# Hybrid GDN/SSD decoder layer in float32: the first SSD group's gate projection is traced amid the keys, the first pair's z projection amid that group's x tiles

## The chip, the cores and the metric

The kernel runs on one core of a Trainium2 chip. A core has a matrix engine (TensorE, PE in the profile; PEld are its weight loads), a vector engine (VectorE, DVE), an activation engine (ScalarE, ACT), GpSimd (POOL), a queue engine (SyncE, SP) that issues the transfers, and 16 DMA engines. The metric is the device time of one execution in microseconds (us).

## The reference, cut to what matters

One decoder layer, batch 1, 1024 tokens, width 1024, all float32. One input projection feeds two token mixers side by side.

```
h = rms_norm(x, pre_mix_norm)
q, k, v, z_a, b_a, a_a, z_s, x_s, b_s, c_s, dt_s = split(h @ w_in)      # 8 GDN heads, 16 SSD heads in 2 groups
q, k, v = silu(causal_conv4(q|k|v)); q, k = l2norm(q)*dk**-0.5, l2norm(k)
o_a = rms_norm(gdn_chunked(q, k, v, g, beta)) * silu(z_a)               # delta rule: a triangular solve per chunk
x_s, b_s, c_s = silu(causal_conv4(x_s|b_s|c_s) + bias)
y = (ssd_chunked(x_s, dt, -exp(a_log), b_s, c_s) + d * x_s) * silu(z_s) # chunked scan, per group
x = x + rms_norm(concat(o_a, rms_norm(y)) @ w_out, post_mix_norm)
h = rms_norm(x, pre_ffn_norm)
gate, up = split(causal_conv3(h @ w_up) + bias)
x = x + rms_norm((silu(gate) * up) @ w_down, post_ffn_norm)
```

## The kernel before

**Projections.** Tokens are done in two halves of 512 (`half`). Every large product is made of three passes: weights and activations are split into a rounded part (`hi`) and a rest (`lo`), and `product3` (L138 to 142) issues hi times hi, hi times lo and lo times hi. One projection of 128 channels over 512 tokens (`project`) is 8 row blocks times 3, so 24 matmuls of 512 columns. `weights` loads 512 KB (SP), makes `whi` (ACT, L127) and `wlo` (DVE, L128; two pieces each); these instructions are traced with a priority that lies 100 places ahead. `conv_proj` is a projection followed by the causal convolution (`conv`, L248: three DVE instructions, and three of ACT around them). `rowwise` is the other form: four accumulators, one for each 128 tokens, and 512 channels at once, so 96 matmuls and four loads of 512 KB. It has no convolution.

**Order.** A main stream (`in_projections`) runs as a generator. Each `yield` of the stream lets every waiting side task (a list `tasks`) go on by one step: that is a round. Between two yields the stream traces 6 or 9 large matmuls. The side tasks are `k_tok` and `k_inner` (inner products of a pair's keys), `solve` (inversion of the 32 by 32 diagonal blocks, 31 steps of two DVE instructions, L602 and L604, after all four pairs of keys went through DRAM), `ssd_chain` (the SSD group's scan over four chunks), `pair_chain` (a head pair's delta rule over four chunks). `wait(n)` lets n rounds pass. The framework then orders each engine's instructions by priority, which is the order of tracing, but lets a later instruction come forward when, by its own planning, an engine would stand idle and the later one has its operands and buffers. Each engine then executes its list in that fixed order.

**The stream of a half**, before: eight key projections (`keys`, four pairs); then the first SSD group: B, C, four x tiles, and last its gate z (`rowwise`, 512 channels, silu at L802); then the head pairs: q and v of pair 0; q of pair 1, the z projection of pair 0 (`pair_z`, two projections, silu at L658), v of pair 1; z of pair 1; the second SSD group; pairs 2 and 3 likewise. `ssd_chain` is put on the list behind the fourth x tile, before the gate projection is traced.

**Buffers that matter.** Accumulators `acc`: 5 PSUM banks (the gate takes 4 at once); `psm`: 3 PSUM banks for everything small; `kq`: 4 (B and C of a group take one, each head one); `sz` (silu of z): 2, one pair's worth; `xrow`: 4 (the gate takes 2); three `wraw`, and `whi` and `wlo` for two projections. A pair's `sz` is freed when its `pair_chain` has ended (`o.over`), the group's `kq` buffer when its chain has read C for the last time.

Of the kernel before, what the change touches and what calls it, by code (L numbers as in the profile page):

```python
# [39 lines left out]
def hybrid_layer_kernel(  # L40
# [247 lines left out]
    def wait(n):  # L288
        for _ in range(n):
            yield  # L290
# [5 lines left out]
    with ExitStack() as actx:  # L296
# [207 lines left out]
                self.ready = 0  # L504
                self.solved = False

        def keys(h, half, gt, ps):

            ks = Keys()
            pairs = []  # L510
            for pair in range(HG // 2):
                o = Work()
                o.half, o.gt, o.pair, o.ks = half, gt, pair, ks
                o.heads = (2 * pair, 2 * pair + 1)
                o.ssk = sp.tile([P, 2, NC], F32, name="ssk", bufs=4)
                o.nk = sp.tile([P, 2, NC], F32, name="nk", bufs=5)
                o.kt, o.kx = [], [None, None]
                for i, hd in enumerate(o.heads):
                    t = ap.tile([P, T], F32, tag="kT", name="kT", bufs=3)
                    o.kt.append(t)  # L520
                    yield from conv_proj(h, half, COL_K + hd * P, 8 + hd,
                                         [gcw[:, tt, 8 + hd:9 + hd] for tt in range(4)], None, t, ps)
                    ps = None
                    nc.sync.dma_start(ks.kt[hd], t)
                    tasks.append(k_tok(o, i))
                tasks.append(k_inner(o))
                pairs.append(o)
                if half == 0 and pair == 1:
                    empty_images()
            tasks.append(solve(ks))  # L530
            return pairs

# [81 lines left out]
        def pair_q(o, h):  # L614
            ks = o.ks
            o.eq = sp.tile([P, 2, NC], F32, name="eq")
            o.kq, o.ktok, o.sz, o.vt = [], [], [None, None], [None, None]
            o.done = 0
            o.qd = ap.tile([P, 2, NC, P], F32, tag="qd", name="qd", bufs=2)
            for i, hd in enumerate(o.heads):  # L620
                t = ap.tile([P, 2, T], F32, tag="kq", name="kq", bufs=4)
                o.kq.append(t)
                nc.sync.dma_start(t[:, 0, :], ks.kt[hd])
                kx = ap.tile([P, NC, P], F32, tag="ktok", name="ktok", bufs=5)
                nc.sync.dma_start(kx, ks.tok[hd].rearrange("p (c n) -> p c n", c=NC))
                o.ktok.append(kx)
                nc.sync.dma_start(o.qd[:, i], ks.dec[hd].rearrange("p (c n) -> p c n", c=NC))
                yield from conv_proj(h, o.half, COL_Q + hd * P, hd,
                                     [gcw[:, tt, hd:hd + 1] for tt in range(4)], None, t[:, 1, :])
                tasks.append(q_tok(o, i))  # L630
# [146 lines left out]
            o.over = True  # L777


        def ssd_group(h, half, gt, g):  # L780
            o = Work()
            o.half, o.gt, o.g = half, gt, g
            o.bc = ap.tile([P, 2, T], F32, tag="kq", name="bc", bufs=4)
            o.xt = ap.tile([P, NC, 512], F32, tag="b8", name="xt", bufs=1)
            for j, (col, cb) in enumerate(((COL_B, 8), (COL_C, 10))):
                ci = cb + g
                yield from conv_proj(h, half, col + g * P, 24 + ci, [scw[:, tt, ci:ci + 1] for tt in range(4)],
                                     scb[:, ci:ci + 1], o.bc[:, j, :])
            tasks.append(b_tok(o))
            for ct in range(4):  # L790
                ci = 4 * g + ct
                xc = yield from conv_proj(h, half, COL_X + ci * P, 24 + ci,
                                          [scw[:, tt, ci:ci + 1] for tt in range(4)], scb[:, ci:ci + 1], None)
                tasks.append(x_tok(o, ct, xc))
            o.zt = None
            tasks.append(ssd_chain(o))
            zt = [xp.tile([P, 2, 512], F32, tag="xrow", name="zt") for _ in range(NC // 2)]
            zt = [zt[c // 2][:, c % 2, :] for c in range(NC)]
            pz = accumulators()
            yield from rowwise(pz, KD, lambda k: (h[0][k], h[1][k]),  # L800
                               lambda k: w_in[k * P:(k + 2) * P, COL_ZS + g * 512:COL_ZS + (g + 1) * 512],
                               lambda c: S_.activation(zt[c], pz[c], AF.Silu))  # L802
            o.zt = zt
# [14 lines left out]
        def ssd_chain(o):  # L818
# [40 lines left out]
            for c in range(NC):  # L859
                L, xdt, xdd = now  # L860
                cl = slice(c * P, (c + 1) * P)
                zero = half == 0 and c == 0
                if not zero:
                    po = bank()
                    PE.matmul(po, bc[:, 1, cl], St[g], start=True, stop=True)
                    yo = ap.tile([P, 512], F32, tag="ch", name="yo", bufs=2)
                    V.tensor_tensor(heads(yo), heads(po), per_head(gt["eg"], c, 64), ALU.mult)
                    V.tensor_tensor(xt[:, c, :], xt[:, c, :], yo, ALU.add)
                if not (half == NH - 1 and c == NC - 1):
                    pn = bank()  # L870
                    PE.matmul(pn, o.bt[:, c, :], xdd, start=True, stop=True)  # L871
                    if zero:
                        V.tensor_copy(St[g], pn)
                    else:
                        V.tensor_tensor(heads(St[g]), heads(St[g]), per_head(gt["el"], c, 64), ALU.mult)
                        V.tensor_tensor(St[g], St[g], pn, ALU.add)
                yield
                yield from wait(W["s2"])
                pd = bank()
                for hh in range(8):  # L880
                    PE.matmul(pd[:, hh * 64:(hh + 1) * 64], L[:, hh, :], xdt[:, hh * 64:(hh + 1) * 64],  # L881
                              start=True, stop=True)
                V.tensor_tensor(xt[:, c, :], pd, xt[:, c, :], ALU.add)
                if c + 1 < NC:
                    now = prepare(c + 1)
                yield
                yield from wait(W["s3"])
            while o.zt is None:
                yield
            yield from wait(W["zt"])  # L890
# [20 lines left out]
        def in_projections(half, rows, w):  # L911

            pg = acc.tile([P, T], F32, tag="acc", name="acc")
            ps = acc.tile([P, T], F32, tag="acc", name="acc")
            g64 = pg[:2 * NG, :]

            def use(k, hi, lo):
                a, z = k == 0, k == KD - 1
                if a:
                    PE.matmul(g64, wga[:, k, :], hi[k], start=True, stop=False)  # L920
                PE.matmul(pg[:NG, :], wga[:, k, :NG], lo[k], start=False, stop=False)
                if not a:
                    PE.matmul(g64, wga[:, k, :], hi[k], start=False, stop=z)
                product3(ps, w[k][0], w[k][1], hi[k], lo[k], a, z)

            h = yield from transposed(rows, wmix, use)
            nonlocal gcw
            if gcw is None:
                gcw = columns(gcw_rows, "colB")
                gcw = gcw.rearrange("p (t c) -> p t c", c=24)  # L930
            gt = {}
            tasks.append(gates(g64, gt, half))
            yield
            pairs = yield from keys(h, half, gt, ps)
            yield from ssd_group(h, half, gt, 0)
            before = None
            for step in (0, 1, "s1", 2, 3):
                if isinstance(step, int):
                    o = pairs[step]
                    while step > 1 and not pairs[step - 2].over:  # L940
                        yield
                    yield from pair_q(o, h)
                    if before is not None:
                        yield from pair_z(before, h)
                    yield from pair_v(o, h)
                    before = o
                else:
                    yield from pair_z(before, h)
                    before = None
                    yield from ssd_group(h, half, gt, 1)  # L950
            nxt = None, None
            if half + 1 < NH:
                nxt = at_once(normed(x, half + 1))
            yield from pair_z(before, h)
            if half + 1 < NH:
                nxt = nxt, first_weights()
            return nxt
# [143 lines left out]
```

## Time and profile before

| | |
|---|---|
| time, median of 3 runs | 1834.17 us (1829.87 to 1834.7) |
| the profiled execution: its time | 1828.55 us |
| the profiled execution: its span, first to last instruction | 1826.6 us |
| PE busy | 1779.3 us, 97% of the span |
| DVE busy | 1221.5 us, 67% |
| ACT busy | 921.5 us, 50% |
| POOL busy | 384.4 us, 21% |
| mean granted clock of TensorE | 0.992 |

The span is what the trace covers; the execution's own time is 1.95 us more. The first half's keys begin at about 22 us, the second half's at about 478 us; the output projection and the feed-forward part fill the rest of the span from about 870 us. In the rows, "busy" of PE counts overlapping matmuls once, so PE can be 100% busy; the clock column is the mean granted clock as a share of 2.4 GHz, and 0.5 of it is the lower level, 1.2 GHz.

### The profile page before, as it was taken

Reading aid. Unit: us, or ns where it says so; the run is one execution under the profiler, and the core shown is the slowest. Engines: PE = TensorE matmul, PEld = TensorE weight load, DVE = VectorE, ACT = ScalarE, POOL = GpSimd, SP = SyncE. Lnnn points to the kernel's source line nnn. Section 1 sums busy time; section 2 is a strip of 40 time slices with the busy share of each in tenths; the row PEclk is TensorE's granted clock in tenths of the full one; section 3 lists DMA queues with packets and bytes.
Section 4 is the critical chain, followed back from the end, with each engine's and each line's share of the span. In section 5 each row is a group of like instructions: output and inputs, shape, how many; then the busy total and the mean of one; then the engine's idle time right before and its main releaser. Section 6 shows DMA issues by size and latency. Waiting matters only on the chain.

```text
span 1826.6 us, 25536 instructions
## 1 busy us (share of the span) xinstructions
PE 1779.3 (97%) x9166; PEld 1452.5 (80%) x9166; DVE 1221.5 (67%) x2534; ACT 921.5 (50%) x1846; POOL 384.4 (21%) x280
## 2 busy tenths in 40 slices
PE   7899999999999999999999999999999999999998
PEld 5777788788777788888787787888888888888886
DVE  7989766876898976786565578777743276455333
ACT  6764445534883544463344555555532245555322
POOL 0313000200131200110000014555400145555000
PEclk9999999999999999999999999999999999999999
DMA  7774445432575543444356855333343363333232
GB/s 249 249 219 110 129 144 161 131 101 65 174 236 163 133 140 120 151 133 117 104 175 194 283 179 185 104 95 103 104 131 100 88 201 98 99 93 104 92 93 81
DMA packets 289721, 257.01 MB, mean 141 GB/s; under 512 B 37462, under 2 KB 226619, under 8 KB 289595
## 3 DMA queue, kind: packets, MB, share of 16 engines
q1 hardware_dynamic: 289595, 255.39, 45.6%
q8 instruction: 72, 1.18, 0.3%
q14 instruction: 54, 0.44, 0.1%
HBM read 215.30 MB, written 40.04 MB: 140 GB/s over the span
## 4 chain that ended last, share of the span: by engine, by line
PE 82%; DVE 8%; issue 2%; ACT 1%; DMA 1%; POOL 1%; DVEq 0%; SPq 0%; POOLq 0%
PE acc L140 24%; PE acc L142 23%; PE acc L141 23%; DVE cv L248 2%; PE psm L881 1%; DVE wlo L128 1%; PE psm L690 1%; PE psm L702 1%; PE psm L741 1%; PE psm L640 1%; PE psm L730 1%; POOL wlo L128 1%; PE psm L408 1%; PE psm L721 1%; PE psm L871 1%
## 5 line engine op out<-in xcount | busy, mean ns | idle before, releaser
L140 PE MATMUL acc<-hhi,whi 128*128 128x512 f32 x1408 | 568.8, 404 | 2.1 <-ACT whi L127 2.1
L142 PE MATMUL acc<-hhi,wlo 128*128 128x512 f32 x1408 | 554.1, 394 | 1.8 <-POOL wlo L128 1.1
L141 PE MATMUL acc<-hlo,whi 128*128 128x512 f32 x1408 | 553.2, 393 | 0.0
L127 ACT CAST whi<-wraw 128x512 fp32r<-128x512 f32 x536 | 329.6, 617 | 437.8 <-PE acc L142 219.8
L128 DVE TENSOR_TENSOR wlo<-wraw,whi 128x512 fp32r<-128x512 f32 x360 | 252.4, 704 | 241.5 <-ACT whi L127 223.2
L128 POOL TENSOR_TENSOR wlo<-wraw,whi 128x512 fp32r<-128x512 f32 x176 | 242.9, 1381 | 507.7 <-ACT whi L127 495.4
L142 PEld LDWEIGHTS acc<-hhi,wlo 128*128 128x128 f32 x1408 | 264.9, 188 | 59.4 <-DVE wlo L128 2.1
L140 PEld LDWEIGHTS acc<-hhi,whi 128*128 128x128 f32 x1408 | 265.4, 188 | 54.4 <-ACT whi L127 3.1
L141 PEld LDWEIGHTS acc<-hlo,whi 128*128 128x128 f32 x1408 | 265.5, 189 | 51.0 <-issue 1.7
L248 DVE SCALAR_TENSOR_TENSOR cv<-pre,colF,cv 128x512 f32<-128x512 f32 x176 | 175.7, 998 | 94.6 <-ACT cv L246 91.6
L140 PE MATMUL acc<-whi,fhi 128*128 128x512 f32 x352 | 139.2, 395 | 0.0
L141 PE MATMUL acc<-wlo,fhi 128*128 128x512 f32 x352 | 139.2, 395 | 0.0
L142 PE MATMUL acc<-whi,flo 128*128 128x512 f32 x352 | 139.2, 395 | 0.0
L248 DVE SCALAR_TENSOR_TENSOR cv<-pre,colB,cv 128x512 f32<-128x512 f32 x144 | 116.0, 809 | 2.2 <-ACT cv L244 1.4
L765 POOL TENSOR_TENSOR vn<-vn,ro 128x512 f32<-128x512 f32 x16 | 18.5, 1169 | 415.8 <-DVE ro L112 246.5
L140 PE MATMUL acc<-whi,mh 128*128 128x512 f32 x256 | 103.0, 402 | 0.0
L141 PE MATMUL acc<-wlo,mh 128*128 128x512 f32 x256 | 101.5, 397 | 0.0
L142 PE MATMUL acc<-whi,ml 128*128 128x512 f32 x256 | 100.8, 396 | 0.0
L242 ACT COPY pre<-acc 128x512 f32<-128x512 f32 x160 | 92.8, 580 | 1.5 <-PE acc L142 1.4
L970 DVE TENSOR_TENSOR ml<-mr,mh 128x512 fp32r<-128x512 f32 x64 | 44.3, 694 | 59.6 <-ACT mh L969 59.4
L140 PEld LDWEIGHTS acc<-whi,fhi 128*128 128x128 f32 x352 | 66.0, 187 | 16.1
L142 PEld LDWEIGHTS acc<-whi,flo 128*128 128x128 f32 x352 | 66.0, 187 | 15.9
(253 smaller groups left out, 2580.2 us busy)
## 6 DMA issues: line engine op xcount, KB each, us to landing
wraw<-in_w_in_dram SPq DMA_DIRECT2D x104, 512.0 KB, 4.2
wraw<-in_w_up_dram SPq DMA_DIRECT2D x88, 512.0 KB, 4.2
wraw<-in_w_down_dram SPq DMA_DIRECT2D x44, 512.0 KB, 3.6
wraw<-in_w_out_dram SPq DMA_DIRECT2D x32, 512.0 KB, 4.5
mr<-mixd SPq DMA_DIRECT2D x64, 256.0 KB, 3.2
xr<-in_x_dram SPq DMA_DIRECT2D x16, 512.0 KB, 5.3
L<-rowsd SPq DMA_DIRECT2D x16, 512.0 KB, 3.7
xr<-x1d SPq DMA_DIRECT2D x16, 512.0 KB, 5.3
```

What stands on the lines that cost most here:

```text
L127: S_.copy(hi, part)
L128: (eng or low[0]).tensor_tensor(lo, part, hi.bitcast(F32), ALU.subtract)
L140: PE.matmul(ps, ahi, bhi, start=first, stop=False)
L141: PE.matmul(ps, ahi, blo, start=False, stop=False)
L142: PE.matmul(ps, alo, bhi, start=False, stop=last)
L242: S_.copy(pre[:, n:n + T], ps)
L248: V.scalar_tensor_tensor(cv, pre[:, t:t + T], w[t], cv, ALU.mult, ALU.add)
L408: PE.transpose(ps[:, c * P:(c + 1) * P], src[:, c * P:(c + 1) * P], ident)
L640: PE.matmul(ps[:, cl], o.kq[i][:, 0, cl], o.kq[i][:, 1, cl], start=True, stop=True)
L690: PE.matmul(p1[d, m, :], at[u, m, d], Xb[u, m, u], start=True, stop=True)
L765: G.tensor_tensor(ot[i], ot[i], ro[:, :, None].broadcast_to([P, NC, P]), ALU.mult)
L970: V.tensor_tensor(ml, mr, mh.bitcast(F32), ALU.subtract)
```

## The change

No instruction is added or taken away; the order of tracing changes. `ssd_group` is split: `ssd_z` is the gate projection by itself, and `keys` calls it for group 0 after its second pair. The z projection of pair 0 goes into the first SSD group, ahead of its third x tile. Where buffers could run out, the stream now waits: the second pair's q waits until the first SSD group's scan is through (`o0.over`, set behind the loop over chunks), and the second pair's z until pair 0 has ended.

```diff
-        def keys(h, half, gt, ps):
+        def keys(h, half, gt, ps, o0):
...
                 if half == 0 and pair == 1:
                     empty_images()
+                if pair == 1:
+                    yield from ssd_z(o0, h)
             tasks.append(solve(ks))
...
-        def ssd_group(h, half, gt, g):
+        def ssd_group(o, h, between=None):
...
             for ct in range(4):
+                if ct == 2 and between is not None:
+                    yield from between
                 ci = 4 * g + ct
...
-            o.zt = None
             tasks.append(ssd_chain(o))
+            if o.zt is None:
+                yield from ssd_z(o, h)
+
+        def ssd_z(o, h):
...
                     now = prepare(c + 1)
                 yield
                 yield from wait(W["s3"])
+            o.over = True
             while o.zt is None:
                 yield
...
-            pairs = yield from keys(h, half, gt, ps)
-            yield from ssd_group(h, half, gt, 0)
+            o0 = ssd_work(half, gt, 0)
+            pairs = yield from keys(h, half, gt, ps, o0)
+            pairs[0].sz = [None, None]
+            yield from ssd_group(o0, h, pair_z(pairs[0], h))
             before = None
             for step in (0, 1, "s1", 2, 3):
                 if isinstance(step, int):
                     o = pairs[step]
-                    while step > 1 and not pairs[step - 2].over:
+                    while step and not (pairs[step - 2] if step > 1 else o0).over:
                         yield
                     yield from pair_q(o, h)
-                    if before is not None:
+                    if step:
+                        o.sz = [None, None]
+                    if before is not None and before.pair:
                         yield from pair_z(before, h)
                     yield from pair_v(o, h)
                     before = o
                 else:
+                    while not pairs[before.pair - 1].over:
+                        yield
                     yield from pair_z(before, h)
                     before = None
-                    yield from ssd_group(h, half, gt, 1)
+                    yield from ssd_group(ssd_work(half, gt, 1), h)
```

## Rows read from the trace of the kernel before

**Rows 1.** The page: busy time of each engine, then the granted clock by slices.

```profile
PE 1779.3 (97%) x9166; PEld 1452.5 (80%) x9166; DVE 1221.5 (67%) x2534; ACT 921.5 (50%) x1846; POOL 384.4 (21%) x280
PEclk9999999999999999999999999999999999999999
```

**Rows 2.** Windows: stretch, length, busy us of PE, PEld, DVE, ACT, POOL; clock; DMA.

```profile
24.00:57.00 33.00, 33.00 (x166) 26.98 (x165) 25.90 (x65) 26.49 (x62) 4.57 (x4) 1.00 0.85 278
57.00:79.00 22.00, 17.43 (x76) 14.22 (x76) 21.25 (x53) 15.58 (x38) 8.50 (x8) 0.84 0.68 234
79.00:124.00 45.00, 45.00 (x226) 37.62 (x225) 37.93 (x101) 39.11 (x76) 12.11 (x11) 1.00 0.80 251
124.00:147.00 23.00, 20.45 (x89) 16.70 (x88) 19.22 (x46) 5.20 (x9) 5.95 (x2) 0.85 0.44 138
147.00:213.00 66.00, 63.30 (x330) 50.24 (x329) 63.27 (x153) 36.24 (x57) 13.58 (x6) 1.00 0.43 108
...
518.00:540.00 22.00, 19.04 (x95) 15.66 (x95) 20.35 (x47) 17.11 (x41) 8.87 (x8) 0.92 0.75 263
...
580.00:600.00 20.00, 16.67 (x85) 13.18 (x86) 19.27 (x37) 5.27 (x10) 5.60 (x3) 1.00 0.27 79
```

**Rows 3.** Timeline of PE: instructions before which it stood idle (start, us, idle before).

```profile
61.77 2.08 PE L577 MATMUL psm<-kT 128*128 128x128 f32 x8 [3.40 <-DVE ast L578]
77.09 0.66 PE L408 MATMUL psm<-ident,kT 128*128 128x128 f32 x4 [1.17 <-ACT kT L400]
...
137.52 1.10 PE L871 MATMUL psm<-xdd,bt 128*128 128x512 f32 x2 [2.55 <-DVE xdd L850]
...
520.18 1.16 PE L577 MATMUL psm<-kT 128*128 128x128 f32 x8 [2.16 <-DVE ast L578]
...
581.50 1.10 PE L871 MATMUL psm<-xdd,bt 128*128 128x512 f32 x2 [2.15 <-DVE xdd L850]
594.87 1.10 PE L871 MATMUL psm<-xdd,bt 128*128 128x512 f32 x2 [1.83 <-DVE xdd L850]
```

**Rows 4.** Timeline of PE in the keys: first and last of 25 successive large matmuls.

```profile
29.76 0.39 PE L142 MATMUL acc<-hhi,wlo 128*128 128x512 f32 x1
...
35.20 0.39 PE L142 MATMUL acc<-hhi,wlo 128*128 128x512 f32 x1
```

**Rows 5.** Timeline of DVE ahead of the idle PE at 61.77 us.

```profile
58.95 0.96 DVE L110 SCALAR_TENSOR_TENSOR rq_a<-xk,rq_y 128x8 f32<-128x8 f32 x1
...
60.35 0.17 DVE L110 SCALAR_TENSOR_TENSOR rq_a<-xk,rq_y 128x8 f32<-128x8 f32 x1
...
61.03 1.28 DVE L578 TENSOR_TENSOR ast<-psm,dd 128x512 f32<-128x512 f32 x2
```

**Rows 6.** Timeline of POOL at the same time.

```profile
57.85 2.04 POOL L572 TENSOR_TENSOR dd<-dd,sc 128x512 f32<-128x512 f32 x2
```

**Rows 7.** Groups of DVE instructions, 24 to 255 us (count, busy us, mean ns, idle before).

```profile
L128 DVE TENSOR_TENSOR wlo<-wraw,whi 128x512 fp32r<-128x512 f32 x58 | 39.4, 684 | 12.6 <-ACT whi L127 10.8 <-PE psm L902 1.6
L248 DVE SCALAR_TENSOR_TENSOR cv<-pre,colB,cv 128x512 f32<-128x512 f32 x48 | 38.5, 807 | 0.4 <-DMA ktd<-kT 0.3
L834 DVE TENSOR_SCALAR L<-L,cs 128x128 f32<-128x128 f32 x48 | 14.9, 337 | 0.0
...
L846 DVE TENSOR_TENSOR L<-L,cb 128x1024 f32<-128x1024 f32 x4 | 4.9, 1215 | 0.0
...
L850 DVE TENSOR_TENSOR xdd<-xdt,edl 128x512 f32<-128x512 f32 x4 | 2.7, 681 | 0.0
```

**Rows 8.** Groups of DVE instructions, 84 to 180 us: the solve's two lines.

```profile
L604 DVE TENSOR_TENSOR xi<-xi,tmpx 128x31 f32<-128x31 f32 (+15 forms) x31 | 11.5, 370 | 0.2
L602 DVE TENSOR_TENSOR tmpx<-at,xi 128x31 f32<-128x31 f32 (+15 forms) x31 | 10.6, 342 | 0.2
```

**Rows 9.** Timeline of DVE: the solve's first and last product, first half.

```profile
126.15 0.18 DVE L602 TENSOR_TENSOR tmpx<-at,xi 128x31 f32<-128x31 f32 x1
175.55 0.18 DVE L602 TENSOR_TENSOR tmpx<-at,xi 128x31 f32<-128x31 f32 x1
```

**Rows 10.** Timeline of SP: the last key stored, then the solve's four reads.

```profile
93.19 0.38 SPq L524 DMA_DIRECT2D ktd<-kT  x1
...
110.55 4.62 SPq L593 DMA_DIRECT2D at<-atd  x4
```

**Rows 11.** Windows: the stretch of the second SSD group's scan, first half.

```profile
310.00:375.00 65.00, 64.20 (x330) 52.22 (x328) 53.77 (x116) 33.95 (x63) 16.36 (x10) 1.00 0.46 142
```

More of the change, by code (lines that the diff above doesn't have):

```diff
@@ L616, in pair_q @@
             o.eq = sp.tile([P, 2, NC], F32, name="eq")
-            o.kq, o.ktok, o.sz, o.vt = [], [], [None, None], [None, None]
+            o.kq, o.ktok, o.vt = [], [], [None, None]
             o.done = 0
@@ L777, in pair_chain, with ssd_work @@
             o.over = True
-        def ssd_group(h, half, gt, g):
+        def ssd_work(half, gt, g):
             o = Work()
-            o.half, o.gt, o.g = half, gt, g
+            o.half, o.gt, o.g, o.zt = half, gt, g, None
+            return o
+        def ssd_group(o, h, between=None):
+            half, gt, g = o.half, o.gt, o.g
             o.bc = ap.tile([P, 2, T], F32, tag="kq", name="bc", bufs=4)
@@ L794, in ssd_group @@
                 tasks.append(x_tok(o, ct, xc))
-            o.zt = None
             tasks.append(ssd_chain(o))
+            if o.zt is None:
+                yield from ssd_z(o, h)
+        def ssd_z(o, h):
+            g = o.g
             zt = [xp.tile([P, 2, 512], F32, tag="xrow", name="zt") for _ in range(NC // 2)]
```

## Prediction

> **What bounds the kernel now.** I read the page first: PE is busy for 97% of the span, so the sum of its matmuls is the floor, and no edit that only reorders can take any of them away [rows 1]. What can be had is PE's idle time and the time it spends at the lower clock. Windows over both halves' input projections show where that lies [rows 2]. In the first half PE loses nothing from 24 to 57 us. It loses 22.00 - 17.43 = 4.6 us from 57 to 79, the later keys, where the clock is 0.84. It loses 2.6 us from 124 to 147, where the clock is 0.85, and 2.7 us from 147 to 213. A stretch with the clock at 0.84 for 22 us has lost a further 22 x 0.16 = 3.5 us of matmul time. The reader is to see in the same rows that DVE is busy for 21.25 of 22.00 us and 63.27 of 66.00 us in two of these stretches, and only 84% of the stretch between them: PE idles where DVE has no room left.
>
> PE's own timeline names what it waited for [rows 3]. There are two kinds. In the keys (61.77 and 520.18 us) it waits 3.40 and 2.16 us at the matmul of `k_inner` for a PSUM bank that DVE's `ast` (L578) has to empty. By the stream's order this is the second pair's `k_inner`, traced beside the third pair's projections, just where the change puts the gate. In the SSD scan (137.52, 581.50 and 594.87 us) it waits 2.55, 2.15 and 1.83 us for `xdd` (L850) from a DVE that runs the solve and the scan at once. The lower clock follows the stalls: 0.84 in the window of the first, 0.85 in that of the scan's first, 0.92 at 518 to 540 [rows 2].
>
> **The change part by part.** No instruction and no transfer is added or removed; PE's sum stays. What each moved part brings with it:
>
> *The gate amid the keys.* Twenty-four successive starts of large matmuls take 35.20 - 29.76 = 5.44 us, 0.227 us each [rows 4]. So a projection is 5.44 us of PE and the gate, with 96 matmuls, 21.8 us. On DVE a key projection costs two `wlo` of 0.684 us and three convolution steps of 0.807 us, 3.8 us in all, before `k_inner` [rows 7]. The gate has eight `wlo` and no convolution: 5.5 us of DVE beside 21.8 us of PE. It is thus 16 us of matmuls in which DVE can catch up, at the place where it was full. I take the stall at 61.77 us, its lower clock, and the ACT-ended wait at 77.09 us behind DVE's convolutions as gone: 3.40 + 3.5 + 1.17 = 8.1 us. In the second half 2.16 us and the clock at 0.92 for 22 us (1.76 us) go: 3.9 us. The gain is 12.0 us. The other bound is a gain of nothing, if what stalls there is not load (below).
>
> The gate's four loads of 512 KB are issued on SP amid the keys' own stores. They keep the pace of projections, 512 KB for every 5.44 us of PE, in stretches where DMA stands at 0.68 to 0.85 [rows 2]; I cost them at nothing, since PE lost no time at 0.85 from 24 to 57 us. Its four accumulators leave one bank for the next key; the gate gives them back one by one as `rowwise` sorts its last matmuls by chunk, so nothing is costed there either. Two of the four `xrow` buffers are held longer; nobody asks for them until the next group.
>
> *Pair 0's z amid the x tiles.* Two projections, 10.9 us of PE with 4 x 0.684 = 2.7 us of DVE. After the last key is stored at 93.19 us the solve's reads are issued at 110.55 us and its first product runs at 126.15 us: 33 us of latency, mostly not of DVE [rows 9, 10]. From 79 to 124 us PE is full already [rows 2]. So this cover goes where none was missing, and leaves the place where pair 1 used it.
>
> *What the cover is taken from.* The solve takes 11.5 + 10.6 = 22.1 us of DVE [rows 8], a chunk of the scan 8 x 0.337 + 1.215 + about seven instructions like L850 of 0.681 us + 0.3 = 9.0 us, so 36 us for four [rows 7]. Before, these 58 us stood beside the gate and pair 0's q and v: 43.6 us of large matmuls with 5.5 + 15.2 us of DVE, 79 us of DVE in all. The solve runs from 126 to 176 us there, over the gate and into the scan [rows 9]. Now the keys end a gate later, the solve starts about 33 us behind them, and the scan starts behind the last x tile. Beside both stand q and v of pairs 0 and 1: the same 43.5 us of matmuls with 30.3 us of DVE, so 88 us. That is 9.7 us more DVE per half against the same matmuls.
>
> *The new waits.* Counting rounds in the code, the scan needs about 32 from its start to `o0.over`, and the stream gives 12 (q and v of pair 0, three each). So some 20 rounds of scan and pair chain are traced with no large matmul between them, and 5 more in front of pair 1's z. Behind the waiting stream stand pair 1's q, v and z. The planner may draw them forward, since their weights, banks and convolution buffers are free; only the second q's `kq` and z's `sz` are not, and those are wanted after the matmuls. The lower bound is the trace's other scan, 310 to 375 us, where a scan runs beside q and v and PE loses 0.8 us of 65 [rows 11]; DVE is at 83% there. The upper bound is all 9.7 us per half exposed. The place is nearer to the stretch from 147 to 213 us, with DVE at 96% and 2.7 us lost. I take 2.7 us per half on top of what that place already loses: 5.4 us. The scan's own stalls (2.55 with its clock, 2.15, 1.83) I leave as they are, at another time.
>
> Sum: -12.0 + 5.4 = -6.6 us. The profiled execution took 1828.55 us, which would make it 1822.0; the median of the runs lies 5.6 us above it, and the forecast stands on the median: 1834.2 - 6.6 = 1827.6 us.
>
> *A rule that speaks against the gain.* Just ahead of the idle PE three of DVE's tiny steps, 8 elements wide, take almost 1 us each, as the one at 58.95 us (0.96 us), while POOL multiplies `dd` (57.85 us, 2.04 us for two); as soon as POOL is done the same step takes 0.17 us at 60.35 us, and then `ast` runs at 61.03 us [rows 5, 6]. The Trainium skill, page "SBUF — State Buffer", section "Who interferes with whom", says that DVE and GpSimd share one pair of ports under an exclusive lock, and that a DVE instruction with two SBUF inputs waits for a GpSimd instruction that reads SBUF. This trace agrees: 0.96 against 0.17 us. By that rule the stall is not one of load, and the first term is 2.2 us in place of 12.0, as the second rival works out.
>
> **The rivals.**
>
> *The cover is missed where it was taken (slower).* The place is the 20 rounds behind pair 0's v. Price: the whole 9.7 us in both halves, 19.4 us, and a stretch at the lower clock in each, 3.5 us as at 124 to 147 us [rows 2]: 26.4 us. Less the keys' 12.0 that is +14.4 us, 1848.6 us. For it: DVE at 96% already, with 9.7 us more to come. Against it: 10.9 us of pair 1's z stand ready to be drawn forward. It decides from the point where PE loses 6 us more per half there than before.
>
> *The keys' stall is contention, not load (no change).* POOL's multiplications and the tiny steps stay where they are; three steps at 0.96 instead of 0.17 us make 2.4 of the 3.40 us, and in the second half all 2.16. Only 1.0 + 1.17 = 2.2 us are won, and the clock is not. With 0.8 to 2.7 us per half lost at the new waits the time is 1833.6 to 1837.4 us. For it: the rows of DVE and POOL. Against it: PE's list now has the gate's matmuls at this place, and DVE, with less queued, comes to `ast` earlier.
>
> *The scan's stalls go too (faster still).* If DVE, relieved in the keys, is through with the third and fourth pair earlier and the solve is spread out, 2.55 + 3.45 + 2.15 + 1.83 = 10.0 us more go and the waits cost nothing: 1834.2 - 22.0 = 1812 us. Against it: solve and scan still fall together.
>
> **How the numbers follow.** Chances: my forecast 0.44, its own range 1821 to 1833; slower by missed cover 0.26; contention 0.20; everything gone 0.10. A measurement of this kernel tells about 0.3% from no change, 5.5 us. Of the forecast's 0.44, 0.33 lie below 1828.7 us; with 0.10 that is 0.43 faster. Of missed cover 0.25 and of contention 0.05 lie above 1839.7 us: 0.30 slower. The rest is 0.27. The range goes from the best case at 1812 us to 1846 us, just short of the slower rival's full price, which assumes both halves exposed in full.
>
> **What would show it.** In the profile after: no idle PE over 1 us at L577 in the keys and a clock of 1.00 there, with DVE well under 97% while the gate runs, would bear out the first term; tiny steps of 1 us followed by the same idle time would bear out contention. PE's idle time and the clock between the last x tile and pair 1's z price the new waits: about 5 us of idle time in the first half if I am right, 12 us or more if the slower rival is. I am wrong altogether if large matmuls of pair 1 are not found among the scan's, or if the stretch from 255 us to the half's end, which I take as unchanged, moves by more than 2 us.

## The result, and the profile after

The changed kernel took 1851.63 us (median of six runs, 1844.66 to 1854.08), the kernel before 1832.36 us beside it: a ratio of 1.01, 95% interval 1.0079 to 1.0122. That is slower by 19.3 us where 6.6 us less was forecast. The profiled execution took 1848.0 us, its span is 1846.3 us and its mean granted clock 0.987 (before 0.992). The numbers of lines have moved: the scan's matmul of `xdd` is now L883 (L871), `k_inner`'s matmul L579 (L577), `ast` L580 (L578).

The page of the kernel after, the lines that answer to [rows 1]:

```profile
PE 1785.3 (97%) x9166; PEld 1457.7 (79%) x9166; DVE 1236.7 (67%) x2534; ACT 906.5 (49%) x1834; POOL 369.9 (20%) x280
PEclk9999899999999989999999999999999999999999
...
L142 PE MATMUL acc<-hhi,wlo 128*128 128x512 f32 x1408 | 555.8, 395 | 9.2 <-DVE wlo L128 8.4
```

PE, DVE and POOL run as many instructions as before. ACT runs twelve fewer, all of them table loads (42, before 54), so "no instruction is added or taken away" holds for the program's own instructions only. The last line is the one to see: 8.4 us of PE's idle time stand ahead of large matmuls whose `wlo` comes late from DVE. Next the windows of the kernel after, in the columns of [rows 2], three stretches of the second half last:

```profile
24.00:57.00 33.00, 31.83 (x163) 25.80 (x162) 25.82 (x65) 26.11 (x64) 3.96 (x3) 1.00 0.82 266
57.00:79.00 22.00, 18.59 (x83) 15.59 (x82) 18.53 (x53) 11.88 (x22) 7.65 (x7) 0.92 0.71 235
79.00:124.00 45.00, 44.86 (x222) 37.36 (x221) 34.29 (x71) 31.47 (x74) 11.05 (x10) 1.00 0.70 228
...
150.00:183.00 33.00, 32.92 (x173) 27.43 (x172) 32.87 (x77) 15.51 (x29) 4.82 (x3) 1.00 0.30 83
183.00:210.00 27.00, 16.92 (x63) 11.05 (x62) 21.98 (x41) 6.17 (x10) 4.36 (x4) 0.81 0.57 134
210.00:260.00 50.00, 47.96 (x351) 39.29 (x350) 41.77 (x128) 29.61 (x68) 5.05 (x4) 1.00 0.47 143
...
628.00:655.00 27.00, 17.54 (x75) 11.97 (x74) 26.03 (x47) 7.15 (x12) 8.19 (x5) 0.79 0.54 122
655.00:712.00 57.00, 54.85 (x380) 45.06 (x380) 42.56 (x126) 34.78 (x73) 4.74 (x4) 0.98 0.47 142
...
730.00:888.00 158.00, 157.91 (x914) 130.26 (x914) 115.65 (x241) 74.06 (x157) 17.30 (x10) 0.98 0.42 127
```

The keys are relieved: DVE is busy for 18.53 of 22.00 us from 57 to 79, not 21.25. Yet PE still loses 3.41 us there. The loss sits from 183 to 210 us: 10.1 us idle, at a clock of 0.81; 628 to 655 repeats it with 9.5 us at 0.79. Behind these places 2.04 us (210 to 260) and 2.15 us (655 to 712) are idle too. Before, PE was idle for 2.55 + 2.70 = 5.25 us in the first half's scan [rows 2] and for 4.33 us in the second's (580 to 655 us), and for nothing behind them up to 260 and 730 us. So PE's idle time there grew by about 7 us in each half.

The page says the same of the whole. The span less PE's busy time is 61.0 us, before 47.3: of the 19.7 us by which the span grew, 13.7 are idle time. The other 6.0 us are PE's busy time, which grew though the 9166 matmuls are the same: they ran longer at the lower clock. PE's timeline of the kernel after names the waits, as [rows 3] did:

```profile
63.02 3.41 PE L579 MATMUL psm<-kT 128*128 128x128 f32 x16 [3.41 <-DVE ast L580]
...
196.51 2.04 PE L883 MATMUL psm<-xdd,bt 128*128 128x512 f32 x2 [3.99 <-DVE xdd L862]
202.32 0.80 PE L142 MATMUL acc<-hhi,wlo 128*128 128x512 f32 x1 [3.77 <-DVE wlo L128]
...
646.25 1.23 PE L883 MATMUL psm<-xdd,bt 128*128 128x512 f32 x2 [2.77 <-DVE xdd L862]
652.06 0.80 PE L142 MATMUL acc<-hhi,wlo 128*128 128x512 f32 x1 [4.58 <-DVE wlo L128]
```

And DVE's timeline shows why the `wlo` at 201.59 us came so late; it is the first of pair 1's q:

```profile
195.31 1.15 DVE L862 TENSOR_TENSOR xdd<-xdt,edl 128x512 f32<-128x512 f32 x1
...
200.51 1.15 DVE L862 TENSOR_TENSOR xdd<-xdt,edl 128x512 f32<-128x512 f32 x1
201.59 2.48 DVE L128 TENSOR_TENSOR wlo<-wraw,whi 128x512 fp32r<-128x512 f32 x4
```

From 182.46 to 201.59 us DVE works without a gap on the scan, the solve's last copy and pair 0's work, and pair 1's four `wlo` stand behind all of it in its list. PE has the weights' upper halves: between 183.19 and 184.29 us it runs four of the 48 large matmuls of pair 1's q, two of hi times hi and two of hi times lo, then none until 202.32. So large matmuls of pair 1 were at hand, much as the slower rival's counter-argument said, but DVE's order kept them shut.

### The profile page after: what moved, and what is told of

The parts are those of the page before. It is cut to its first block, busy times and chain, and to the rows that moved or that the text cites. A ratio compares the mean times of both kernels' runs of the same rounds, so it can differ in the third digit from the quotient of the medians.

```text
span 1846.3 us, 25518 instructions
## 1 busy us (share of the span) xinstructions
PE 1785.3 (97%) x9166; PEld 1457.7 (79%) x9166; DVE 1236.7 (67%) x2534; ACT 906.5 (49%) x1834; POOL 369.9 (20%) x280
## 4 chain that ended last, share of the span: by engine, by line
PE 60%; DVE 2%; issue 1%; POOL 1%; ACT 1%; DMA 0%; DVEq 0%; POOLq 0%
PE acc L140 18%; PE acc L142 18%; PE acc L141 18%; POOL wlo L128 1%; PE psm L893 1%; PE psm L704 1%; PE psm L692 0%; PE psm L743 0%; PE psm L723 0%; PE psm L223 0%; PE psm L642 0%; PE psm L732 0%; PE psm L745 0%; DVE wlo L128 0%; PE psm L741 0%
## 5 line engine op out<-in xcount | busy, mean ns | idle before, releaser
L128 DVE TENSOR_TENSOR wlo<-wraw,whi 128x512 fp32r<-128x512 f32 x360 | 258.4, 721 | 231.4 <-ACT whi L127 217.8
L142 PEld LDWEIGHTS acc<-hhi,wlo 128*128 128x128 f32 x1408 | 266.4, 189 | 67.2 <-DVE wlo L128 10.9
L141 PEld LDWEIGHTS acc<-wlo,fhi 128*128 128x128 f32 x352 | 66.0, 187 | 16.0
```

Source lines behind the costliest of these rows:

```text
L128: (eng or low[0]).tensor_tensor(lo, part, hi.bitcast(F32), ALU.subtract)
L141: PE.matmul(ps, ahi, blo, start=False, stop=False)
L142: PE.matmul(ps, alo, bhi, start=False, stop=last)
```

## The experiments

**The two moves apart.** *e3* moves the gate alone and *e4* z alone; both keep the new wait ahead of pair 1's q. Against the kernel after:

```diff
 e3
-            pairs[0].sz = [None, None]
-            yield from ssd_group(o0, h, pair_z(pairs[0], h))
+            yield from ssd_group(o0, h)
...
-                    if before is not None and before.pair:
+                    if before is not None:
 e4
-                if pair == 1:
-                    yield from ssd_z(o0, h)
```

> One part alone: the gate amid the keys, pair 0's z where it was before (between q and v of pair 1), with the wait for the first scan. Theory 1: the hole behind v of pair 0 is as in the changed kernel, since q of pair 1 is still traced behind the scan: 1845 to 1855 us. Theory 2: the hole shrinks by what z covers, 10.9 us of matmuls a half against 2.7 us of DVE: 1830 to 1840 us.

> The other part alone: pair 0's z amid the x tiles, the gate behind the fourth x tile as before, with the new waits. The gate's 16 rounds and q and v of pair 0 feed the scan again, so the wait is short. Theory 1: no hole of several us, 1830 to 1838 us. Theory 2: the same DVE work against 10.9 us less cover a half: 1838 to 1850 us.

The gate alone took 1878.33 us (ratio 1.0256, 1.0238 to 1.0273), z alone 1819.77 us (0.9936, 0.9918 to 0.9954). Neither fell where it was expected: the gate alone is slower than both of its theories, z alone faster than both of its own. With the wait in place the two edits are of opposite sign, and z alone beats both kernels. Windows of z alone:

```profile
124.00:150.00 26.00, 25.71 (x126) 21.04 (x125) 23.39 (x53) 9.42 (x16) 5.12 (x2) 1.00 0.37 115
150.00:180.00 30.00, 30.00 (x152) 24.05 (x151) 30.00 (x68) 14.95 (x25) 6.71 (x4) 1.00 0.57 133
180.00:210.00 30.00, 27.95 (x158) 21.83 (x157) 26.19 (x63) 15.67 (x27) 3.73 (x2) 1.00 0.38 122
```

DVE is full from 150 to 180 us and PE loses nothing: the last third of the gate's matmuls (32 of 96) stands there until about 160 us, then head projections. With the gate taken away (e3) PE is busy for 27.01 of the 33 us from 150 on, at a clock of 0.93, and for 18.07 of the next 27 at 0.70.

The gain was measured again (*e11*, the same kernel):

> The kernel with z alone moved, a second time on another day of the chip and in more rounds: 1819.8 us plus or minus 3, a ratio of 0.991 to 0.996 to the kernel before, if the gain is one of the kernel and not of that call.

It took 1821.34 us, ratio 0.9950 (0.9932 to 0.9968).

**z's place.** *e8* is z alone, but z comes behind all four x tiles, with the scan's task already begun:

```diff
-                if ct == 2 and between is not None:
-                    yield from between
...
             tasks.append(ssd_chain(o))
+            if between is not None:
+                yield from between
```

> Pair 0's z neither amid the x tiles nor in pair 1, but between the fourth x tile and the gate, behind the point where the scan is put on the list. If z amid the x tiles won because it holds the scan back by 10.9 us of matmuls, so that less of it falls together with the solve on DVE, the win is lost: 1828 us or more. If it won because the scan has more matmuls beside it and pair 1's z no longer holds two accumulators, the win stays or grows: 1812 to 1824 us.

It took 1845.76 us (1.0067, 1.0042 to 1.0091), 24 to 26 us more than z alone, for the place of 10.9 us of matmuls. The solve's products on DVE and the scan's weight loads on PE (nanoseconds, then first and last start), first in z alone, then in e8:

```profile
L602 DVE TENSOR_TENSOR tmpx<-at,xi x31: 172/350/426, 120.5 to 166.7; 128x31 f32<-128x31 f32 x2, 128x60 f32<-128x60 f32 x2, 128x87 f32<-128x87 f32 x2, 128x112 f32<-128x112 f32 x2
...
L881 PEld LDWEIGHTS psm<-xdd,bt x8: 186/189/190, 146.0 to 188.1; 128*128 128x128 f32 x8
```

```profile
L602 DVE TENSOR_TENSOR tmpx<-at,xi x31: 181/357/418, 127.3 to 176.1; 128x31 f32<-128x31 f32 x2, 128x60 f32<-128x60 f32 x2, 128x87 f32<-128x87 f32 x2, 128x112 f32<-128x112 f32 x2
...
L881 PEld LDWEIGHTS psm<-xdd,bt x8: 186/189/190, 141.4 to 183.7; 128*128 128x128 f32 x8
```

Amid the x tiles z holds the scan back and lets the solve run ahead: they share DVE for 166.7 - 146.0 = 20.7 us, in e8 for 34.7, in the kernel before for 175.55 - 137.52 = 38.0 us [rows 3, 9]. PE's idle time over the scan goes roughly with it: 2.3 us from 124 to 210 in z alone, 6.2 in e8, 5.25 to 213 us before. In e8 the scan's stalls are back, 2.77, 1.64 and 1.41 us ahead of `xdd` in the first half; in z alone one of 1.73 us is left, at 188.0 us, and that one waits for `eq`. These stalls are a part only of e8's loss: PE idles for 56.2 us in all there and for 42.6 in z alone, and e8 is 12 us slower than the kernel before with slightly less overlap. The rest of it was not traced.

**The wait ahead of pair 1's q.** *e1* (both moves), *e6* (gate alone) and *e7* (z alone) take away the wait for `o0.over`. Since the four `kq` buffers are then still held by the scan, pair 1's second head takes its tile from another pool, so these three differ in that too:

```diff
-                t = ap.tile([P, 2, T], F32, tag="kq", name="kq", bufs=4)
+                t = xp.tile([P, 2, T], F32, tag="xrow", name="kq") if o.pair * 2 + i == 3 else \
+                    ap.tile([P, 2, T], F32, tag="kq", name="kq", bufs=4)
...
-                    while step and not (pairs[step - 2] if step > 1 else o0).over:
+                    while step > 1 and not pairs[step - 2].over:
```

> The changed kernel, but pair 1's q no longer waits in the tracing for the first scan; its second head's tile, which was what made the wait needed, lies in a free xrow buffer. The work and the place of the gate and of pair 0's z stay. Theory 1 (order): the 20 rounds without large matmuls put the scan's DVE work ahead of pair 1's wlo in DVE's fixed list, and PE has nothing to issue. Then the two stretches with about 10 us of idle time and 5 to 7 us of lost clock per half largely go: 1825 to 1836 us. Theory 2 (load): DVE is full from 150 to 202 us whatever the order, and PE must wait for it: still 1845 us or more.

> The gate amid the keys alone, pair 0's z between q and v of pair 1 as before, and pair 1's q without its wait in the tracing (its second tile in an xrow buffer). Against the run with the wait (1878 us) this prices the wait. Theory 1 (order): the hole behind pair 0's v goes, 1830 to 1842 us. Theory 2 (the gate's cover is missed at the scan whatever the order): 1855 us or more.

> Pair 0's z amid the x tiles alone, and pair 1's q without its wait. With the gate still behind the x tiles the wait lasts few rounds. Theory 1: no difference to the run with the wait (1819.8 us), 1816 to 1824 us. If the wait costs wherever it stands: 1808 to 1815 us.

Medians and ratios of the seven kernels to the kernel before:

| moved | pair 1's q waits | it doesn't |
|---|---|---|
| nothing | (no such wait) | 1.0 |
| z | 1819.77 us, 0.9936; again 0.9950 | 1831.35 us, 0.9997 (0.9982 to 1.0013) |
| gate | 1878.33 us, 1.0256 | 1850.89 us, 1.0092 (1.0066 to 1.0118) |
| both | 1851.63 us, 1.01 | 1837.97 us, 1.0033 (1.0021 to 1.0046) |

So 14 of the change's 19 us go with the wait (12 by the ratios), but only with the gate gone: with z alone the kernel that waits is the faster one, by 10 to 12 us, and without the wait z's move gains nothing. No expectation of e7 had that. Its overlap of solve and scan is that of z alone (solve 121.3 to 167.6 us, first weight load of the scan at 146.8), and from 124 to 210 us PE idles for 3.45 us, 1.1 more. What is lost comes behind, in pair 0's chain (a window of e7, then of z alone, then e7's wait):

```profile
210.00:260.00 50.00, 47.53 (x409) 39.21 (x408) 31.16 (x78) 23.70 (x53) 0.00 (x0) 0.97 0.39 114
210.00:255.00 45.00, 44.94 (x407) 37.80 (x405) 32.67 (x92) 22.32 (x56) 0.00 (x0) 1.00 0.53 156
239.57 0.46 PE L742 MATMUL psm<-y,qd 128*128 128x128 f32 x2 [2.47 <-DVE mts L916]
```

The gain of z alone is thus one of z's place and the wait together. The kernel before with the wait alone was not run, so their shares stay open.

e1 came out 2 us above its range for order, e6 between its two, nearer to that for missed cover. In e1 the stretch that lost 10.1 us loses nothing, and part of it comes back later, in pair 0's chain:

```profile
183.00:210.00 27.00, 27.00 (x133) 21.27 (x132) 26.25 (x52) 15.17 (x25) 6.19 (x5) 1.00 0.59 148
210.00:260.00 50.00, 46.01 (x400) 37.34 (x398) 34.45 (x86) 20.86 (x52) 2.86 (x3) 0.90 0.37 110
```

Two more tell what in the wait does it. *e2* leaves it and puts the `wlo` of pair 1's two q on POOL, out of DVE's list; *e9* lets the first of the two q be traced ahead of the wait, in its own buffer.

```diff
 e2, in pair_q
-                                     [...], None, t[:, 1, :])
+                                     [...], None, t[:, 1, :], eng=G if o.pair == 1 else None)
 e9
+                while i and until is not None and not until.over:
+                    yield
...
-                    while step and not (pairs[step - 2] if step > 1 else o0).over:
+                    while step > 1 and not pairs[step - 2].over:
                         yield
-                    yield from pair_q(o, h)
+                    yield from pair_q(o, h, o0 if step == 1 else None)
```

> The changed kernel with its wait, but the rest wlo of pair 1's two q projections is made on POOL in place of DVE (8 instructions in all). Theory 1, in its narrow form (PE lacks only wlo, which stands behind the scan on DVE): most of the 10 us of idle time per half go, 1826 to 1838 us. If the late tracing itself holds back pair 1's q (loads, banks, ACT), or DVE's load is what counts (5.5 us less DVE work would give at most 5 us): 1844 us or more.

> The kernel after, but of pair 1's two q projections only the second waits for the scan's end; the first is traced before it, so that its four wlo stand ahead of most of the scan in DVE's list. Theory (the loss is one of order: matmuls whose wlo stands behind the scan can't cover the scan): the wlo wait at 202 us goes, PE has 5.4 us more of large matmuls beside the scan in each half, and of the 14 us that the whole wait costs some 5 to 10 us come back: 1841 to 1847 us. Rival (only the whole absence of the wait helps, since it is the length of the waiting that counts): within 3 us of the kernel after, 1849 to 1854 us.

e2 took 1845.18 us (1.0066, 1.0045 to 1.0087), e9 1842.79 us (1.0061, 1.0040 to 1.0082): 6 and 9 of the 14 us come back (6 and 7 of 12 by the ratios). The stretch in e2, then in e9, and what is left in e9:

```profile
183.00:210.00 27.00, 25.25 (x108) 18.82 (x107) 27.00 (x46) 11.93 (x19) 8.64 (x6) 0.94 0.62 145
183.00:210.00 27.00, 20.26 (x82) 14.73 (x81) 23.94 (x48) 8.24 (x13) 4.78 (x4) 0.80 0.42 94
```

```profile
207.12 0.79 PE L142 MATMUL acc<-hhi,wlo 128*128 128x512 f32 x1 [4.30 <-DVE wlo L128]
```

In e2 no wait for `wlo` over 0.9 us is left in either half, and this stretch idles for 1.75 us instead of 10.1. Its time is nevertheless in the range that was set for its rivals (1844 us or more): PE's idle time falls by 6.7 us over the span, but busy time grows by 6.9 as more of it runs at the lower clock (0.86 from 210 to 260 us), in a profiled execution that is the slowest of its five. In e9 the first q covers part of the scan, and the wait for `wlo` has moved to the second q, which still stands behind the scan. I had expected it to vanish; here it moves to the projection that is first behind the wait. That the order in DVE's list makes the wait for `wlo` is shown by both; that it is all of the 14 us is not.

**The keys' stall.** *e5* is the kernel before with `dd` multiplied on DVE; the others are z alone with one edit: *e14* multiplies on ACT, *e10* starts the gates' task two rounds earlier, *e12* traces the products two rounds ahead of the matmuls, *e13* lets the chain run two rounds longer before both.

```diff
 e5 (e14: four S_.activation(..., AF.Copy, scale=sc[:, i, c:c + 1]))
-                G.tensor_tensor(dd[:, i], dd[:, i], sc[:, i, :][:, :, None].broadcast_to([P, NC, P]), ALU.mult)
+                V.tensor_tensor(dd[:, i], dd[:, i], sc[:, i, :][:, :, None].broadcast_to([P, NC, P]), ALU.mult)
 e10: g=5 -> g=3 in W;  e13: inner=4 -> inner=6 in W
 e12
+            yield
+            yield
+            for i, hd in enumerate(o.heads):
                 ps = bank()
```

> The kernel before, with k_inner's product of dd and sc (eight instructions a half) on DVE in place of POOL. The stall of 3.40 us in the keys came back in the changed kernel to a hundredth of a us, with the gate beside it. If it is a chain of latencies through POOL and DVE's tiny steps held up by POOL (rival 2 of the prediction), it shrinks to under 1.5 us and its lower clock goes: 1825 to 1831 us, though DVE has 5 us more work a half. If it is DVE's load, it grows: 1834 us or more.

> The kernel with z alone moved (1819.8 us), with the number of rounds that the gates' task waits cut from 5 to 3, so that the first pair's chain of dd, select, exponential and product starts earlier against the same matmuls. Theory (the keys' stall is the length of that chain, started late): the stall of 3.40 us at 62.2 us shrinks or goes, with 3.4 us of lower clock at most, 1813 to 1818 us. Rival (the stall is DVE's load or sits where the bank is asked for, whatever the chain's start): the stall stays over 2.5 us and the time within 2 us of 1819.8 us.

> The kernel with z alone moved (1819.8 and 1821.3 us in two sets of runs); in k_inner the two products of dd with sc are traced two rounds ahead of the two matmuls that fill a PSUM bank each, instead of each product just ahead of its matmul. Theory (banks are held idle through a long chain, from 50.1 to 62.3 us): the stall of 3.40 us goes to under 1 us in the first half and that of 2.20 us in the second, 1812 to 1818 us. Rival (the wait follows ast wherever the matmul stands, or another task is made late instead): a stall over 2 us stays in the keys, time within 3 us of 1820.5 us.

> The kernel with z alone moved, with the rounds that k_inner waits between the exponential and its products raised from 4 to 6, so that products, matmuls and ast all come two rounds later. Theory (banks held through the chain): the matmuls come when the exponential is nearer to its end, the stall shrinks by half or more, 1813 to 1819 us. Rival (POOL's products and DVE's tiny steps under POOL's lock make it, wherever they stand): a stall over 2 us stays, at a later time, time within 3 us of 1820.5 us; later keys could also hold the solve up and cost 2 to 5 us.

> The kernel with z alone moved (1819.8 and 1821.3 us), with the products of dd with sc on ACT, four instructions of 128 columns for each head, in place of POOL. Theory (POOL's product slows DVE's tiny steps and ast behind them): the steps take 0.17 us each, ast runs 2 us earlier and the keys' stall shrinks from 3.40 to under 1.5 us; ACT has about 2.5 us more per pair, 1815 to 1821 us. Rival (the chain of subtraction, select and exponential sets ast's time, whoever multiplies): the steps are fast, but the stall stays over 2.5 us, time within 3 us of 1820.5 us or later, if ACT's casts for the projections are held up.

| | us | ratio | keys' first stall |
|---|---|---|---|
| e5 | 1833.39 | 1.0001 (0.9986 to 1.0016) | 2.79 at `ast` |
| e10 | 1822.22 | 0.9945 (0.9927 to 0.9962) | 3.09 at `ast` |
| e12 | 1830.54 | 0.9992 (0.9976 to 1.0008) | 3.05 at the next key's `kT` |
| e13 | 1825.28 | 0.9948 (0.9931 to 0.9966) | 3.05 at the next key's `kT` |
| e14 | 1834.73 | 1.0030 (1.0014 to 1.0047) | 1.78 at `ast` |

On the stall e10 and e13 came out by their rivals (over 2 us of it stay), e5 and e14 between theory and rival. In e12 the matmul of `k_inner` no longer waits, but the next key does, by as much:

```profile
63.13 1.16 PE L580 MATMUL psm<-kT 128*128 128x128 f32 x8
68.04 0.66 PE L408 MATMUL psm<-ident,kT 128*128 128x128 f32 x4 [3.05 <-ACT kT L400]
```

Neither range of e12 held its time, 1830.54 us. Taking the banks later does not help: the wait goes on to the next work behind `ast`, a `kT` that ACT makes from a convolution of DVE. In e14, where POOL doesn't multiply, the small steps of DVE that stood beside the product are fast and the stall is halved (DVE's and PE's timelines):

```profile
57.94 0.17 DVE L112 SCALAR_TENSOR_TENSOR rq_y<-rq_a,rq_y 128x8 f32<-128x8 f32 x1
58.14 0.17 DVE L110 SCALAR_TENSOR_TENSOR rq_a<-xk,rq_y 128x8 f32<-128x8 f32 x1
```

```profile
60.16 1.16 PE L578 MATMUL psm<-kT 128*128 128x128 f32 x8 [1.78 <-DVE ast L579]
```

About 1.6 of the 3.40 us thus go with POOL's multiplication: two steps of 0.98 and 0.96 us (57.94 and 58.95 us in the kernel before) now take 0.17 each. A third slow step does not stand beside the product. In the kernel before it is this one, beside POOL's select, and e14 still has it at 1.05 us:

```profile
56.85 1.05 DVE L111 TENSOR_TENSOR rq_a<-rq_a,rq_y 128x8 f32<-128x8 f32 x1
```

```profile
56.39 1.49 POOL L552 TENSOR_SCALAR_AFFINE_SELECT dd<-dd 128x1024 f32<-128x1024 f32 x1 [1.21 <-DVE dd L550]
```

The other 1.8 us stay open: the chain of subtraction, select and exponential ahead of `ast` is a candidate that no run isolated. None of the five gained on the kernel it starts from. e14 has eight more instructions a pair on ACT in place of POOL's two, and a new wait of 2.66 us for the next pair's `ast` at 76.76 us (z alone: 1.99 us there, for a `kT`); what else makes it slower was not traced.

## Why the prediction was wrong

*The gain in the keys (12.0 us) is the first step that failed.* It took the stall at 61.77 us "as gone", because DVE was full there and the gate gives it 16 us of room. DVE got that room, 18.53 of 22.00 us, and the stall came back at 3.41 us, behind the same two steps of 0.98 and 0.96 us. A wait of 1.17 us for a `kT` is still there, now at 56.20 us. In the second half 2.16 us became 2.09 us, now ahead of a key's transposes. So nothing of the idle time was won. By the prediction's own count of the clock 3.5 - 1.76 us in the first half and 1.76 us in the second were won, 3.5 us in all instead of 12.0.

The rival of contention was right that the stall would stay, and had the rows for it. That its 2.2 us are near the 3.5 is luck: it had idle time won and the clock not, and it came out the other way round. Its price for the steps was also too high. It read three steps as standing beside POOL's product; two do, the third stands beside the select, and e14 gives 1.6 us where it had 2.4. The rule of the Trainium skill that the prediction weighed there (page "SBUF — State Buffer", section "Who interferes with whom") agrees with e14's 0.17 us beside no work of POOL against 0.98 and 0.96 us beside its product.

*The new waits (5.4 us) are the second.* With both moves made, the wait ahead of pair 1's q alone costs 13.7 us (1851.63 against 1837.97 us in e1), and PE's idle time behind pair 0's v grew by about 14 us over both halves. The step that failed is "the planner may draw them forward, since their weights, banks and convolution buffers are free". A large matmul also needs its `wlo`, and DVE's list had that behind the scan. The prediction counted q, v and z of pairs 0 and 1 as cover by their length, not by the place of their first DVE instruction. Of the 48 large matmuls of pair 1's q four were drawn forward.

By the runs the miss splits so. Without the wait (e1) the two moves cost 4.6 us where 12.0 were to be won, 16.6 us off; the wait cost 13.7 where 5.4 were reckoned, 8.3 us off. Together that is 24.9 of the 25.9 us between forecast and result. Of the 16.6 the keys make 8.5. The other 8 have no single wait: in e1's profile PE is idle for 1.4 us more than before, and its busy time is 8.1 us longer (1787.4 us), at the lower clock.

*"This cover goes where none was missing" is the third.* z's move is no neutral term: with the gate moved it takes 27 us off with the wait (e3 against the kernel after) and 13 without it (e6 against e1); with the gate in its old place and no wait it changes nothing (e7). What the traces show it to do is to delay the scan's start, from 137.5 to 146.0 us in z alone, while the solve, its reads issued at 110.47 us as before [rows 10], starts at 120.5 instead of 126.2 us. The prediction had seen that solve and scan fall together, and left it as a reason against the fastest rival. That this overlap sets the time is not shown: e7 has as little of it as z alone and is no faster than the kernel before.

*The slower rival came nearest.* Its place (between pair 0's v and pair 1's z) is right, its time, 1848.6 us, is near the 1851.6 measured, and from 150 to 260 us PE idles 0.08 + 10.08 + 2.04 = 12.2 us, over the 12 it named. Its mechanism holds in part: it priced 9.7 us a half of DVE's load against the same matmuls, but in e1, with the cover just as far away, the stretch from 183 to 210 us loses nothing. It left out the order of `wlo`, which made its counter-argument ("10.9 us of pair 1's z stand ready") worthless. The nearness has luck in it too: it took 12.0 us off for the keys that were not won.

*What held:* that PE gets no more matmuls; that SP's moved loads cost nothing (while the gate runs, from 56.6 to 80 us, the only wait of PE over 0.9 us is the one for `ast`); and that the stretch from 255 us on hardly moves: from the first product of pair 1's chain to that of the half's last chain it was 184.2 us, and is 186.1.

## What to carry to other kernels

Price cover by what each covering matmul must still wait for, in the list of the engine that makes it ready: a projection whose weight split stands behind the scan covers nothing of the scan. Try the parts of a change apart, and each with and without the waits that it needs: z's move won 10 to 14 us with the wait and nothing without it, while the gate, cover with little DVE work (21.8 us of PE with 5.5 us of DVE), cost 17 to 45 us when it alone was taken from the solve's side, and won some 3.5 us in the keys. A full engine ahead of a stall is no proof of load: look first at whether its small instructions take longer than elsewhere.

## What was not expected of the hardware

The lower clock came in one piece after a long wait. Windows of the kernel after, before, in and behind it:

```profile
186.00:196.50 10.50, 5.20 (x30) 3.37 (x28) 10.50 (x23) 3.70 (x5) 2.88 (x2) 1.00 0.82 203
196.60:206.80 10.20, 6.43 (x13) 3.89 (x14) 7.69 (x14) 0.24 (x1) 1.04 (x1) 0.50 0.24 62
206.80:210.00 3.20, 3.20 (x16) 2.64 (x15) 0.69 (x1) 0.84 (x2) 0.00 (x0) 1.00 0.46 136
```

PE was busy for half of 10.50 us, and the following 10.20 us ran at 0.50, the level of 1.2 GHz, though large matmuls stood back to back from 202.91 us on; 647.0 to 657.3 us is the same at 0.51. By the prediction's count (length times lost clock) that piece is 5.1 us, where it had reckoned 3.5; but PE was busy for only 6.43 of the 10.20 us, so some 3.2 us of matmul time were lost in it. Nor does the length of a wait alone set what follows: behind the same wait of 3.4 us in the keys the clock from 57 to 79 us was 0.84 before and 0.92 after.

And POOL slows more of DVE's instructions than the 8-wide ones: in e10 a 128x128 step of the scan took four times as long while POOL multiplied `dd`, on DVE's timeline, with POOL's product below:

```profile
58.15 1.07 DVE L844 TENSOR_SCALAR L<-L,cs 128x128 f32<-128x128 f32 x1
...
62.44 0.27 DVE L844 TENSOR_SCALAR L<-L,cs 128x128 f32<-128x128 f32 x1
```

```profile
58.09 2.04 POOL L572 TENSOR_TENSOR dd<-dd,sc 128x512 f32<-128x512 f32 x2
```
